# Half of a merge gate by seven block products, woven into the chunks of the next projection

## The chip, the cores and the metric

One core of a Trainium2 chip runs the whole kernel. The metric is the device time of one execution in microseconds, as a median of several. TensorE (PE in the profile, with PEld for its weight loads) multiplies; VectorE (DVE), ScalarE (ACT) and GpSimd (POOL) do the rest; SyncE (SP) issues most transfers, POOL those that add to what lies in SBUF.

## What is computed

One layer of an encoder block, 256 tokens, width 2048, float32:

```python
z = xn @ w_in[l]
u_lru, g_lru, q, k, v, g_attn, m_lru, m_attn = jnp.split(z, split_at, axis=-1)
...
y_a = h.astype(x.dtype) * jax.nn.silu(g_lru)
...
y_b = windowed_gqa(q, k, v, attn_sink[l]) * jax.nn.silu(g_attn)
merged = (jax.nn.sigmoid(m_lru) * (y_a @ w_proj_a[l])
          + jax.nn.sigmoid(m_attn) * (y_b @ w_proj_b[l]))
x = x + rms_norm(merged @ w_out[l], norm_post_w[l])
```

All matrices are 2048 high; w_in is 13312 wide, the others 2048. The change concerns m_attn, the attention's merge gate, which are the last 2048 columns of w_in.

## The kernel before, in words

Every float32 operand of a product is split into a high part rounded to fp32r (wh, written by ScalarE) and a low part, the rest (wl, by VectorE); a product is then three matmuls, high by high, high by low, low by high (`mm3`, L228 to L230). The weights come from DRAM in pieces of 128x2048 (1024 KB), one per step. `load_plan` lists the steps in order. A step has two half steps, each with one 128x1024 half of a piece.

Four kinds of steps there are. A "quad" is a quarter of the 2048 rows for a chunk of 512 output columns: 24 matmuls of 128x512 for the 256 tokens (`add_rows`). A "blk" makes columns on partitions (`add_pair`). A "part" is a step of the seven products: a 2x2 block of matrices is multiplied with seven products of sums of blocks instead of eight products of blocks (`Seven`, table `SEVEN`). Here the rows of the blocks are the two halves of the tokens (or of the 2048 inner rows, as pairs of 128), the columns two neighbouring chunks of 512. Each product has two steps of 12 matmuls. So 1024 output columns are 8 quads (192 matmuls) or 14 parts (168).

A product of seven needs sums on both sides. Sums of the left operand's blocks are made by VectorE (`sums_of`: four sums s1 to s4 of a pair unit, in fp32r parts of 128x4x2x128). Sums of the weights are made by transfers: a cell in SBUF is loaded with one block (`start`, by SP), and further blocks are added into it by POOL's accumulating transfers (`second`, and for m6, m7 and m4 in `fetch`, five steps ahead of use). Blocks are only added there; what has to be subtracted is in the left operand's sums and in the last additions (`after`). The products m1 and m2 use plain blocks, loaded like any other piece.

The order of the work is the order in which the code records it, half step by half step, in the loop at the end of `body`. At half step n the loop issues transfers (`fetch`, three steps ahead), runs what is due there (`at`, `soon`), splits the high part four half steps ahead and the low part three ahead (`split`), runs `behind` work, and records the half step's matmuls. Each engine then takes its own instructions in that order and waits by semaphores. Pieces have 3 buffers (raw), split halves 5, so ScalarE's cast for half step n+4 waits until TensorE has done half step n-1. Larger tiles share 34 slots of 4 KB per partition (`unit`).

The stages, in order: the inner branches' inputs (u, gl, ga) with the recurrence, k and v, then the heads stage: per group of four heads two q pairs and one chunk of MID (ml's second half and w_proj_a), while scores, softmax and values of the group before are woven in. After that comes the gate stage: four chunks of ma (m_attn, `gate_evac` applies the sigmoid) and four of pb (w_proj_b, `add_pb`). After a pb chunk VectorE multiplies by the gate and adds the other branch, two `turn`s transpose the result on TensorE, and its parts and their sums are made for w_out. w_out's stage takes its first two chunks by seven products, woven with the quads of chunks 2 and 3 in the order of `OUT`.

The lines that the prediction speaks of: L211 raw loads, L190 adding transfers and L192 plain cell loads, L223 high parts, L225 low parts, L313 to L315 sums, L156 low parts of activations, L785 to L806 softmax and transposes of p, L855 and L856 the evacuation of pb, L867 transposes of a turn.

Of the kernel before, what the change touches and what calls it, by code (L numbers as in the profile page):

```python
# [14 lines left out]
F32 = mybir.dt.float32  # L15
F32R = mybir.dt.float32r
AF = mybir.ActivationFunctionType
ALU = mybir.AluOpType
# [37 lines left out]
}  # L56


OUT = ("2.0 m1.0 2.1 m1.1 2.2 m5.0 m5.1 m3.0 2.3 m3.1 m6.0 m6.1 3.0 m2.0 m2.1 m7.0 3.1 m7.1 m4.0 m4.1 3.2 3.3").split()


PV_NORM = 0
# [9 lines left out]
def load_plan():  # L72

    plan = []

    def quad(m, c):
        plan.extend(("quad", m, c, i) for i in range(4))

    def pair(m, c, n):
        plan.extend(("blk", m, c + (n + i) * P, 0) for i in range(2))  # L80

    def mixed(m, c, order):
        for o in order:
            a, i = o.split(".")
            plan.append(("part", m, c, a, int(i)) if a in SEVEN else ("quad", m, c + int(a) * 512, int(i)))

    quad("w_in", U0)
    for i in range(8):
        if i in EARLY:
            quad("w_in", ML0 + EARLY.index(i) * 512)  # L90
        pair("w_in", GL0, 2 * i)
        pair("w_in", GA0, 2 * i)
        if i < 6:
            pair("w_in", U0, 2 * i + 4)
    pair("w_in", K0, 0)
    pair("w_in", K0, 2)
    quad("w_in", V0)
    for i in range(4):
        pair("w_in", Q0, 4 * i)
        pair("w_in", Q0, 4 * i + 2)  # L100
        quad(*MID[i])
    for m, c in MID[4:]:
        quad(m, c)
    for c in range(4):
        quad("w_in", MA0 + c * 512)
    for c in range(4):
        quad("w_proj_b", c * 512)
    mixed("w_out", 0, OUT)
    return plan

# [13 lines left out]
def body(ctx, tc, x, xT, wall, wlru, pvec, npost, ident_d, mask_d, rope_d, out):  # L124
# [3 lines left out]
    ring = ctx.enter_context(tc.tile_pool(name="ring", bufs=3))  # L128
    small = ctx.enter_context(tc.tile_pool(name="small", bufs=2))
    psum = ctx.enter_context(tc.tile_pool(name="psum", bufs=4, space=PSUM))  # L130
    ctx.enter_context(tc.manual_schedule())

    def unit(name, dt=F32, shape=(P, 4, S)):
# [5 lines left out]
    def banks(name, shape=(P, 2, 2, S)):  # L139
        return psum.tile(list(shape), F32, tag="mm", name=name, bufs=2)  # L140

    def half_unit(name, tag, dt=F32, bufs=2):
        return small.tile([P, 2, S], dt, tag=tag, name=name, bufs=bufs)
# [21 lines left out]
    def at(hs, fn):  # L165
        assert hs >= now[0], (hs, now[0])
        due.setdefault(hs, []).append(fn)
# [3 lines left out]
    def behind(hs, fn):  # L171
        last[hs] = fn
# [4 lines left out]
    def soon(fn, d=1):  # L177
        at(now[0] + d, fn)
# [125 lines left out]
    def sums_of(name, src, sums, psum):  # L304
        a = src.rearrange("p a b -> p (a b)")
        a11, a12, a21 = (a[:, i * P:(i + 1) * P] for i in (0, 2, 1))
        ends = src.rearrange("p a (b c) -> p (a b) c", b=2)[:, 0:4:3]
        f = half_unit(f"{name}f", "uu", F32).rearrange("p a (b c) -> p (a b) c", b=2)
        t = unit(name, F32R, (P, 4, 2, P))
        sums.append(t)  # L310

        def make(a21):
            nc.vector.tensor_tensor(f[:, 0:2], ends, a21.unsqueeze(1).to_broadcast([P, 2, P]), ALU.subtract)  # L313
            nc.vector.scalar_tensor_tensor(f[:, 2], f[:, 1], -1.0, a11, ALU.mult, ALU.subtract)
            nc.vector.scalar_tensor_tensor(f[:, 3], f[:, 2], -1.0, a12, ALU.mult, ALU.subtract)  # L315
            soon(lambda: parts_of(t[:, :, 0], t[:, :, 1], f))

        if psum:

            nc.scalar.copy(f[:, 3], a21)  # L320
            soon(lambda: make(f[:, 3]))
        else:
            make(a21)

    class Seven:

        def __init__(self, name, m, c, act, sums, done):
            self.name, self.act, self.sums, self.done = name, act, sums, done  # L330
            self.weights, self.cells, self.ps = ("part", m, c), {}, {}
            groups[m, c] = self

# [19 lines left out]

        def half(self, m, q, h, wh, wl):
            fresh, last = q == 0 and h == 0, q == 1 and h == 1
            if fresh and m in ("m5", "m3"):

                if m == "m5":
                    self.double = banks(f"{self.name}{m}", (P, 2, 512))
                self.ps[m] = self.double[:, int(m == "m3")]  # L360
            elif fresh:
                self.ps[m] = bank(f"{self.name}{m}", (P, 512))
            for j in range(2):
                ah, al = self.rows(SEVEN[m][0], 4 * q + 2 * h + j)
                sl = slice(j * 512, (j + 1) * 512)
                mm3(self.ps[m], ah, al, wh[:, sl], wl[:, sl], fresh and j == 0, last and j == 1)
            if last:
                soon(lambda: self.after(m))
# [4 lines left out]
        def after(self, m):  # L373
            ps, done = self.ps, self.done
            if m == "m1":
                self.m1 = small.tile([P, 512], F32, tag="upad", name=f"{self.name}c", bufs=2)
                nc.scalar.copy(self.m1, ps.pop("m1"))
            elif m == "m2":
                done(0, 0, ps.pop("m2"), self.m1, 1)
            elif m == "m6":  # L380

                self.u = self.temp("u")
                nc.vector.tensor_tensor(self.u, ps.pop("m6"), self.m1, ALU.add)
                v = self.temp("v")
                nc.vector.tensor_tensor(v, ps["m5"], self.u, ALU.add)
                done(0, 1, ps.pop("m3"), v, -1)
            elif m == "m7":

                nc.vector.tensor_tensor(self.u, ps.pop("m7"), self.u, ALU.add)
                done(1, 1, ps.pop("m5"), self.u, -1)  # L390
            elif m == "m4":
                done(1, 0, ps.pop("m4"), self.u, 1)
# [299 lines left out]
            scaled(dst, ps, lambda: soon(sigmoid))  # L692
        return done

    tm, sm, ms, msum = {}, {}, [], []


    def gate_evac(gates, c):
        def done(t, ps):
            if c not in gates:  # L700
                gates[c] = unit(f"mg{c}", F32, (P, 2, 512))
            nc.scalar.activation(gates[c][:, t], ps, AF.Sigmoid, scale=rtok[:, t:t + 1])
        return done
# [127 lines left out]
    def yb_parts(q):  # L831
        yb[q] = pair_unit(f"yb{q}")
        n = q % 2 * 2
        parts_of(yb[q][:, :, 0], yb[q][:, :, 1], sga[q // 2][:, n:n + 2])

    def heads(g):
        def then(h, l):
            b = now[0] + HEAD0
            for j in range(4):
                if j % 2 == 0:  # L840
                    both = {}
                head(4 * g + j, h, l, b + 4 * j, both)
        return then
# [8 lines left out]
    def add_pb(c):  # L852
        def done(t, ps):
            g = sm[c][:, t]
            nc.vector.tensor_tensor(g, ps, g, ALU.mult)  # L855
            nc.vector.tensor_tensor(g, tm[c][:, t], g, ALU.add)  # L856
            if t == 1:
                for i in range(2):
                    soon(lambda i=i: turn(i), i + 1)

        def turn(i):

            ps = bank(f"mt{c}{i}")
            for j in range(2):
                sl = slice((2 * i + j) * P, (2 * i + j + 1) * P)
                for t in range(2):
                    nc.tensor.transpose(ps[:, j, t * P:(t + 1) * P], sm[c][:, t, sl], ident)  # L867
            m = pair_unit(f"ms{2 * c + i}")
            ms.append(m)
            parts_of(m[:, :, 0], m[:, :, 1], ps)  # L870
            sums_of(f"mx{2 * c + i}", ps, msum, True)

        add_rows(f"pb{c}_", yb, done)

    def add_mixed(seven, order, classic):
        left = {}
        for o in order:
            a, i = o.split(".")
            if a in SEVEN:
                seven.add(a, int(i))  # L880
                continue
            if i == "0":
                n = len(steps)
                classic(int(a))
                left[a] = steps[n:]
                del steps[n:]
            steps.append(left[a].pop(0))
# [10 lines left out]
    for m, c in MID:  # L898
        mid.append((add_pa, c // 512) if m == "w_proj_a" else (add_ml, (c - ML0) // 512))
    for i in range(4):  # L900
        add_heads(f"q{i}", heads(i))
        f, n = mid[i]
        f(n)
    for f, n in mid[4:]:
        f(n)

    b = 2 * len(steps)
    for q in range(8):
        at(b + 12 + q, lambda q=q: yb_parts(q))
    for c in range(4):  # L910
        add_rows(f"ma{c}_", xs, gate_evac(sm, c))
    for c in range(4):
        add_pb(c)


    npt, xr, yw = [], [[], []], [[], []]
# [65 lines left out]
    for q in range(2):  # L982
        at(b - 16 + 4 * q, lambda q=q, s=seven: s.start("x", q))
        at(b - 12 + 4 * q, lambda q=q, s=seven: s.second(q))
        at(b - 4 + 4 * q, lambda q=q, s=seven: s.start("y", q))
    add_mixed(seven, OUT, lambda c: add_rows(f"o{c}_", ms, lambda t, ps: o_done(t, c, ps), c == 3, c == 3))


    assert [s[0] for s in steps] == [p[0] for p in plan]
# [91 lines left out]
```

## Time and profile before

| | |
|---|---|
| median of 3 runs | 904.9 us (904.82 to 905.37) |
| the profiled execution | 905.53 us, span 903.7 us, mean granted clock 0.997 |
| matmuls, busy share of TensorE | 4638, 99% |
| busy share of VectorE, ScalarE | 75%, 61% |
| transfers | 180.59 MB, mean 200 GB/s |
| ma's four chunks | from 633.7 to about 721 us |
| pb's four chunks | from about 723 to 815 us |

The page tells busy times per engine, slices of the span, transfer queues, the chain of waits and the costliest groups. A group's row reads: line, engine, operation, what is written and read, shape and count, then busy time and mean ns, then the idle time before it and who ended it. A windows row gives busy time and count per engine in a stretch, then the clock, the share of the 16 transfer engines and GB/s.

### The profile page before, as it was taken

The numbers are of one execution on the slowest core, as the hardware profiler recorded it, in microseconds if no ns is written. First come the engines' busy times: TensorE is split into PE (matmuls) and PEld (weight loads), VectorE is DVE, ScalarE is ACT, GpSimd is POOL, SyncE is SP. The second block draws the span as 40 slices with busy tenths as digits, with TensorE's granted clock in tenths as the row PEclk, the third lists the DMA queues.
The fourth block names the chain that finished last, engine by engine and source line by source line (L and its number), as shares of the span: only waits on it lengthen the run. The fifth ranks groups of instructions, "written<-read, shape, count | busy, mean of one in ns | idle before, by whom it ended". The sixth has DMA issues, their size and how long they took to land.

```text
span 903.7 us, 12068 instructions
## 1 busy us (share of the span) xinstructions
PE 893.5 (99%) x4638; PEld 765.8 (85%) x4638; DVE 678.0 (75%) x947; ACT 555.5 (61%) x777; POOL 16.8 (2%) x40
## 2 busy tenths in 40 slices
PE   8999999999999999999999999999999999999996
PEld 8888888888898888888888888888888888888885
DVE  6897978696979889896687868656555447778686
ACT  7688586958687977844555544654455444445764
POOL 0000000000000000000000000000000000101200
PEclk9999999999999999999999999999999999999998
DMA  9764555546455454555544444535555556988992
GB/s 339 251 241 170 191 206 198 197 145 212 176 215 196 159 205 150 199 210 187 187 170 157 163 164 141 185 140 186 187 187 186 186 186 227 289 303 274 223 314 93
DMA packets 30778, 180.59 MB, mean 200 GB/s; under 512 B 3424, under 2 KB 4192, under 8 KB 12160
## 3 DMA queue, kind: packets, MB, share of 16 engines
q1 hardware_dynamic: 27840, 170.67, 52.7%
q0 software_dynamic: 2304, 8.39, 4.9%
q10 hardware_dynamic: 576, 0.76, 0.3%
q8 instruction: 36, 0.59, 0.2%
q14 instruction: 22, 0.18, 0.1%
HBM read 177.71 MB, written 2.10 MB: 199 GB/s over the span
## 4 chain that ended last, share of the span: by engine, by line
PE 98%; DMA 0%; DVE 0%; ACT 0%; DVEq 0%; issue 0%; SPq 0%
PE q L255 6%; PE ga L255 6%; PE gl L255 6%; PE u L255 5%; PE gl L253 3%; PE ga L253 3%; PE q L253 3%; PE u_ps L509 3%; PE u L253 3%; PE k L255 2%; PE omm L229 1%; PE omm L230 1%; PE omm L228 1%; PE o L230 1%; PE o L228 1%; PE o L229 1%
## 5 line engine op out<-in xcount | busy, mean ns | idle before, releaser
L223 ACT CAST wh<-raw 128x1024 fp32r<-128x1024 f32 (+1 forms) x299 | 309.0, 1041 | 220.7 <-PE q L255 31.4
L225 DVE TENSOR_TENSOR wl<-raw,wh 128x1024 fp32r<-128x1024 f32 (+1 forms) x300 | 358.3, 1205 | 107.2 <-ACT wh L223 106.3
L255 PE MATMUL q<-xs,wh 128*128 128x512 f32 x256 | 62.8, 391 | 0.0
L255 PE MATMUL ga<-xs,wh 128*128 128x512 f32 x256 | 62.4, 391 | 0.0
L255 PE MATMUL gl<-xs,wh 128*128 128x512 f32 x256 | 62.4, 391 | 0.0
L255 PEld LDWEIGHTS gl<-xs,wh 128*128 128x128 f32 x256 | 46.9, 188 | 9.0
L255 PEld LDWEIGHTS ga<-xs,wh 128*128 128x128 f32 x256 | 46.9, 188 | 8.9
L255 PEld LDWEIGHTS q<-xs,wh 128*128 128x128 f32 x256 | 46.6, 188 | 8.8
L255 PE MATMUL u<-xs,wh 128*128 128x512 f32 x192 | 46.8, 391 | 0.0
L255 PEld LDWEIGHTS u<-xs,wh 128*128 128x128 f32 x192 | 35.2, 188 | 6.7
L253 PE MATMUL q<-xs,wl 128*128 128x256 f32 x256 | 34.4, 284 | 0.0
L253 PEld LDWEIGHTS q<-xs,wl 128*128 128x128 f32 x256 | 33.1, 191 | 1.2
L253 PEld LDWEIGHTS gl<-xs,wl 128*128 128x128 f32 x256 | 33.0, 191 | 1.2
L253 PEld LDWEIGHTS ga<-xs,wl 128*128 128x128 f32 x256 | 33.0, 191 | 1.3
L253 PE MATMUL gl<-xs,wl 128*128 128x256 f32 x256 | 33.7, 283 | 0.0
L253 PE MATMUL ga<-xs,wl 128*128 128x256 f32 x256 | 33.5, 283 | 0.0
L253 PEld LDWEIGHTS u<-xs,wl 128*128 128x128 f32 x192 | 24.8, 191 | 0.9
L253 PE MATMUL u<-xs,wl 128*128 128x256 f32 x192 | 25.2, 283 | 0.0
L608 DVE SCALAR_TENSOR_TENSOR uu<-upad,pv,uu 128x256 f32<-128x256 f32 x48 | 23.3, 485 | 2.3
L785 DVE CUSTOM_DVE_ANT_0 p<-sc,mask,pv 128x256 f32<-128x256 f32 x32 | 14.2, 478 | 9.9 <-PE sc L230 9.7
L631 ACT ACTIVATE gr<-gate,pv 128x256 f32<-128x256 f32 x32 | 15.3, 477 | 4.6 <-PE gate L230 4.6
L230 PE MATMUL gate<-ul,lwl 128*128 128x256 f32 x64 | 18.1, 283 | 0.0
(436 smaller groups left out, 2027.5 us busy)
## 6 DMA issues: line engine op xcount, KB each, us to landing
raw<-wall_dram SPq DMA_DIRECT2D x145, 1024.0 KB, 4.8
lraw<-wlru_dram SPq DMA_DIRECT2D x8, 512.0 KB, 5.7
raw<-wall_dram SPq DMA_DIRECT2D x8, 256.0 KB, 4.5
xr<-x_dram SPq DMA_DIRECT2D x4, 512.0 KB, 12.3
omx0a<-wall_dram POOLq DMA_DIRECT2D x3, 512.0 KB, 6.9
omx0b<-wall_dram POOLq DMA_DIRECT2D x3, 512.0 KB, 8.4
omx1a<-wall_dram POOLq DMA_DIRECT2D x3, 512.0 KB, 9.5
omx1b<-wall_dram POOLq DMA_DIRECT2D x3, 512.0 KB, 11.0
```

The lines of the kernel that those rows point to most:

```text
L223: cast(hs, raw)
L225: nc.vector.tensor_tensor(ls, raw, hs.bitcast(F32), ALU.subtract)
L228: nc.tensor.matmul(ps, wh, xh, start=start, stop=False)
L229: nc.tensor.matmul(ps, wh, xl, start=False, stop=False)
L230: nc.tensor.matmul(ps, wl, xh, start=False, stop=stop)
L253: nc.tensor.matmul(ps[:, 1], wl[:, sl], a[:, 0], start=False, stop=False)
L255: nc.tensor.matmul(ps, wh[:, sl], a, start=k == 0, stop=k == KT - 1)
L509: nc.tensor.matmul(ups[b // 2][:, b % 2, m], w[:, sl], a[:, n], start=k == 0 and w is wh and m == 0, stop=stop)
L608: nc.vector.scalar_tensor_tensor(u, up[:, j, tap:tap + S], cw[:, tap:tap + 1], u, ALU.mult, ALU.add)
L631: nc.scalar.activation(v["gr"][:, 2 * d + j], ps[:, 0], AF.Sigmoid, bias=pv[:, PV_BR + b:PV_BR + b + 1])
L785: nc.vector.tensor_tensor_reduce(p[:, t], sc[:, t], mask[:, t], P ** -0.5, sk, ALU.add, ALU.max, m[:, t:t + 1])
```

## The change

The upper half of m_attn (columns 1024 to 2047, ma's chunks 2 and 3) is now computed with seven products. Its 14 parts are woven with the quads of ma's chunks 0 and 1 and with those of all four pb chunks, in the order of the new list `GATE`. The left operand is x, whose eight pair units xs live through most of the kernel. The sums of their blocks are made in the heads stage (`x_sums`, two per group of heads), stored in DRAM and their slots given back; in the gate stage they are loaded again (`x_sums_back`), four and four. m5 and m3 of this group get a bank each instead of one double bank. The temporary u of `Seven` uses another buffer ring. The turns of pb's chunk 0 come ten half steps later.

```diff
+GATE = ("a0.0 a0.1 m1.0 a0.2 m1.1 a0.3 m2.0 a1.0 m2.1 a1.1 m5.0 m3.0 a1.2 a1.3 b0.0 m6.0 m7.0 b0.1 b0.2 m5.1 m3.1 "
+        "b0.3 b1.0 b1.1 m6.1 m7.1 b1.2 b1.3 b2.0 m4.0 m4.1 b2.1 b2.2 b2.3 b3.0 b3.1 b3.2 b3.3").split()
+CHUNKS = {"a": ("w_in", MA0), "b": ("w_proj_b", 0), "o": ("w_out", 0)}
...
-    for c in range(4):
-        quad("w_in", MA0 + c * 512)
-    for c in range(4):
-        quad("w_proj_b", c * 512)
+    mixed("w_in", MA0 + 1024, GATE)
     mixed("w_out", 0, OUT)
...
+    away = [dram.tile([P, 4 * 2 * P], F32, name=f"away{q}") for q in range(8)]
+    xsum = {}
+
+    def x_sums(q):
+        a = half_unit(f"xa{q}", "uu", F32)
+        nc.vector.tensor_tensor(a, xs[q][:, :, 0].bitcast(F32), xs[q][:, :, 1].bitcast(F32), ALU.add)
+        sums_of(f"xx{q}", a, xsum, False)
+        soon(lambda: nc.sync.dma_start(away[q], xsum.pop(q).rearrange("p a b c -> p (a b c)").bitcast(F32)), 3)
+
+    def x_sums_back(q):
+        xsum[q] = unit(f"xb{q}", F32R, (P, 4, 2, P))
+        nc.sync.dma_start(xsum[q].rearrange("p a b c -> p (a b c)").bitcast(F32), away[q])
...
-                self.u = self.temp("u")
+                self.u = small.tile([P, 512], F32, tag="upad", name=f"{self.name}u", bufs=2)
...
                 for i in range(2):
-                    soon(lambda i=i: turn(i), i + 1)
+                    soon(lambda i=i: turn(i), (10 if c == 0 else 1) + i)
...
     for i in range(4):
+        behind(2 * len(steps) + 14, lambda i=i: x_sums(2 * i))
+        behind(2 * len(steps) + 18, lambda i=i: x_sums(2 * i + 1))
         add_heads(f"q{i}", heads(i))
...
     b = 2 * len(steps)
+    seven = Seven("am", "w_in", MA0 + 1024, xs, xsum, lambda t, c, ps, *a: then(gate_evac(sm, 2 + c), t, combine(f"af{t}{c}", ps, *a)), False)
+    for q in range(2):
+        at(b + 18 * q, lambda q=q, s=seven: s.start("x", q))
+        at(b + 6 + 18 * q, lambda q=q, s=seven: s.second(q))
+        at(b + 10 + 22 * q, lambda q=q, s=seven: s.start("y", q))
     for q in range(8):
-        at(b + 12 + q, lambda q=q: yb_parts(q))
-    for c in range(4):
-        add_rows(f"ma{c}_", xs, gate_evac(sm, c))
-    for c in range(4):
-        add_pb(c)
+        at(b + 14 + q, lambda q=q: yb_parts(q))
+        at(b + 7 + q if q < 4 else b + 30 + q, lambda q=q: x_sums_back(q))
+    add_mixed(seven, GATE, lambda kind, c: add_rows(f"ma{c}_", xs, gate_evac(sm, c)) if kind == "a" else add_pb(c))
```

In the lists, a0.0 is the first quad of ma's chunk 0, b of pb, o of w_out; m5.1 is the second step of product m5.

SP's queue at the start of the gate stage, before: raw pieces, one behind the other.

```order
L211 DMA raw_5909<-wall_dram 128x2048
L211 DMA raw_5948<-wall_dram 128x2048
L211 DMA raw_5984<-wall_dram 128x2048
L211 DMA raw_6025<-wall_dram 128x2048
L211 DMA raw_6064<-wall_dram 128x2048
```

The same place now. amx and amy are the cells of the weights' sums, xb are the sums of x coming back.

```order
L198 DMA amx0a<-wall_dram 128x1024
L198 DMA amx0b<-wall_dram 128x1024
L217 DMA raw_6003<-wall_dram 128x2048
L217 DMA raw_6042<-wall_dram 128x2048
L217 DMA raw_6067<-wall_dram 128x2048
L343 DMA xb_6087<-away_74 128x1024
L217 DMA raw_6112<-wall_dram 128x2048
L343 DMA xb_6114<-away_75 128x1024
L343 DMA xb_6127<-away_76 128x1024
L217 DMA raw_6139<-wall_dram 128x2048
L198 DMA amy0a<-wall_dram 128x1024
L198 DMA amy0b<-wall_dram 128x1024
```

Cells and sums stand between the raw pieces, so a piece goes behind up to three of them.

VectorE behind pb's chunk 1, before: four evacuations (mg), then the two turns (ms, mx) with one split (wl) between them.

```order
L855 TENSOR_TENSOR mg_6182<-pb__6620,mg_6182 128x512
L856 TENSOR_TENSOR mg_6182<-mg_1446,mg_6182 128x512
L225 TENSOR_TENSOR wl_1_6768<-raw_6712,wh_1_6767 128x1024
L225 TENSOR_TENSOR wl_0_6794<-raw_6749,wh_0_6793 128x1024
L156 TENSOR_TENSOR ms_6815<-mt_6810,ms_6815 128x2x256
L313 TENSOR_TENSOR mx2f<-mt_6810,mx2f 128x256
L314 SCALAR_TENSOR_TENSOR mx2f<-mx2f,mt_6810 128x128
L315 SCALAR_TENSOR_TENSOR mx2f<-mx2f,mt_6810 128x128
L225 TENSOR_TENSOR wl_1_6821<-raw_6749,wh_1_6820 128x1024
```

And now:

```order
L162 TENSOR_TENSOR ms_6876<-mt_6871,ms_6876 128x2x256
L319 TENSOR_TENSOR mx1f<-mt_6871,mx1f 128x256
L320 SCALAR_TENSOR_TENSOR mx1f<-mx1f,mt_6871 128x128
L875 TENSOR_TENSOR mg_6444<-pb__6690,mg_6444 128x512
L876 TENSOR_TENSOR mg_6444<-mg_1456,mg_6444 128x512
L231 TENSOR_TENSOR wl_1_6886<-amx0b,wh_1_6885 128x1024
L162 TENSOR_TENSOR mx_6853<-mx0f,mx_6853 128x4x128
L231 TENSOR_TENSOR wl_0_6913<-amx1a,wh_0_6912 128x1024
L162 TENSOR_TENSOR mx_6879<-mx1f,mx_6879 128x4x128
L162 TENSOR_TENSOR ms_6936<-mt_6931,ms_6936 128x2x256
L319 TENSOR_TENSOR mx2f<-mt_6931,mx2f 128x256
L231 TENSOR_TENSOR wl_1_6942<-amx1b,wh_1_6941 128x1024
```

Chunk 0's turns (mx0f, mx1f) end just ahead of chunk 1's evacuation, their low parts stand behind it, and the splits there are m4's, whose half steps have half the matmuls.

VectorE in the heads stage, at the first `x_sums`, has five rows that were not there:

```order
L337 TENSOR_TENSOR xa_4030<-xs_132 128x512
L319 TENSOR_TENSOR xx0f<-xa_4030 128x256
L320 SCALAR_TENSOR_TENSOR xx0f<-xx0f,xa_4030 128x128
L321 SCALAR_TENSOR_TENSOR xx0f<-xx0f,xa_4030 128x128
L231 TENSOR_TENSOR wl_0_4027<-raw_3988,wh_0_4026 128x1024
L162 TENSOR_TENSOR xx_4033<-xx0f,xx_4033 128x4x128
```

They stand behind the splits of a half step; the low part xx follows one split later.

More of the change, by code (lines that the diff above doesn't have):

```diff
@@ L56 @@
 }
-OUT = ("2.0 m1.0 2.1 m1.1 2.2 m5.0 m5.1 m3.0 2.3 m3.1 m6.0 m6.1 3.0 m2.0 m2.1 m7.0 3.1 m7.1 m4.0 m4.1 3.2 3.3").split()
+GATE = ("a0.0 a0.1 m1.0 a0.2 m1.1 a0.3 m2.0 a1.0 m2.1 a1.1 m5.0 m3.0 a1.2 a1.3 b0.0 m6.0 m7.0 b0.1 b0.2 m5.1 m3.1 "
+        "b0.3 b1.0 b1.1 m6.1 m7.1 b1.2 b1.3 b2.0 m4.0 m4.1 b2.1 b2.2 b2.3 b3.0 b3.1 b3.2 b3.3").split()
+OUT = ("o2.0 m1.0 o2.1 m1.1 o2.2 m5.0 m5.1 m3.0 o2.3 m3.1 m6.0 m6.1 o3.0 m2.0 m2.1 m7.0 o3.1 m7.1 m4.0 m4.1 o3.2 o3.3").split()
+CHUNKS = {"a": ("w_in", MA0), "b": ("w_proj_b", 0), "o": ("w_out", 0)}
 PV_NORM = 0
@@ L84, in mixed @@
             a, i = o.split(".")
-            plan.append(("part", m, c, a, int(i)) if a in SEVEN else ("quad", m, c + int(a) * 512, int(i)))
+            if a in SEVEN:
+                plan.append(("part", m, c, a, int(i)))
+            else:
+                w, w0 = CHUNKS[a[0]]
+                plan.append(("quad", w, w0 + int(a[1]) * 512, int(i)))
     quad("w_in", U0)
@@ L130, in body @@
     psum = ctx.enter_context(tc.tile_pool(name="psum", bufs=4, space=PSUM))
+    dram = ctx.enter_context(tc.tile_pool(name="dram", bufs=1, space=bass.MemoryType.DRAM))
     ctx.enter_context(tc.manual_schedule())
@@ L309, in sums_of @@
         t = unit(name, F32R, (P, 4, 2, P))
-        sums.append(t)
+        sums[int(name[2:])] = t
         def make(a21):
@@ L323, in sums_of, with __init__ @@
             make(a21)
+    away = [dram.tile([P, 4 * 2 * P], F32, name=f"away{q}") for q in range(8)]
[8 more added lines that the diff above has]
+        nc.sync.dma_start(xsum[q].rearrange("p a b c -> p (a b c)").bitcast(F32), away[q])
     class Seven:
-        def __init__(self, name, m, c, act, sums, done):
-            self.name, self.act, self.sums, self.done = name, act, sums, done
+        def __init__(self, name, m, c, act, sums, done, double=True):
+            self.name, self.act, self.sums, self.done, self.double = name, act, sums, done, double
             self.weights, self.cells, self.ps = ("part", m, c), {}, {}
@@ L355, in half @@
             fresh, last = q == 0 and h == 0, q == 1 and h == 1
-            if fresh and m in ("m5", "m3"):
+            if fresh and self.double and m in ("m5", "m3"):
                 if m == "m5":
-                    self.double = banks(f"{self.name}{m}", (P, 2, 512))
-                self.ps[m] = self.double[:, int(m == "m3")]
+                    self.pair = banks(f"{self.name}{m}", (P, 2, 512))
+                self.ps[m] = self.pair[:, int(m == "m3")]
             elif fresh:
@@ L693, in silu_evac @@
         return done
-    tm, sm, ms, msum = {}, {}, [], []
+    tm, sm, ms, msum = {}, {}, [], {}
     def gate_evac(gates, c):
@@ L883, in add_mixed @@
                 n = len(steps)
-                classic(int(a))
+                classic(a[0], int(a[1]))
                 left[a] = steps[n:]
@@ L985, in body @@
         at(b - 4 + 4 * q, lambda q=q, s=seven: s.start("y", q))
-    add_mixed(seven, OUT, lambda c: add_rows(f"o{c}_", ms, lambda t, ps: o_done(t, c, ps), c == 3, c == 3))
+    add_mixed(seven, OUT, lambda _, c: add_rows(f"o{c}_", ms, lambda t, ps: o_done(t, c, ps), c == 3, c == 3))
     assert [s[0] for s in steps] == [p[0] for p in plan]
```

## The prediction, made before the result was known

> **What bounds the kernel now.** I read the page's busy times first, then the chain of waits, then the list of TensorE's own waits.
>
> ```profile
> PE 893.5 (99%) x4638; PEld 765.8 (85%) x4638; DVE 678.0 (75%) x947; ACT 555.5 (61%) x777; POOL 16.8 (2%) x40
> PEclk9999999999999999999999999999999999999998
> PE 98%; DMA 0%; DVE 0%; ACT 0%; DVEq 0%; issue 0%; SPq 0%
> PE u_ps L509 <- DVE wh L223: 1.1, 1, 1.1
> PE spin L406 <- POOL eps L402: 1.0, 1, 1.0
> PE u_ps L509 <- DVE xs L436: 0.5, 1, 0.5
> ```
>
> TensorE is busy for 99% of the span and is 98% of the chain. The three rows are all its waits, 2.6 us, and all lie at the start. The clock's digit is 9 in every slice but the last, the tail. So time is the number of products, and a product taken out counts in full as long as nothing else makes TensorE wait. Busy alone doesn't prove that products run at their best rate, so I take the rate from starts:
>
> ```profile
> L228 PE MATMUL ma__6035<-wh,xs x32: 389/389/389, 657.3 to 678.4; 128*128 128x512 f32 x32
> L228 PE MATMUL ma__6339<-wh,xs x32: 389/389/389, 700.8 to 721.9; 128*128 128x512 f32 x32
> 700.00:710.00 10.00, 10.00 (x46) 8.29 (x45) 4.27 (x4) 5.15 (x6) 0.00 (x0) 1.00 0.61 211
> 840.00:850.00 10.00, 10.00 (x46) 8.29 (x45) 6.13 (x5) 5.46 (x7) 3.12 (x4) 1.00 1.06 255
> ```
>
> Two chunks later the same product starts 700.8 - 657.3 = 43.5 us later. That is 192 products, so 226.6 ns each (the 389 ns are overlapped). The last two rows (PE, PEld, DVE, ACT, POOL, clock, DMA share, GB/s) are 10 us of ma's chunks and 10 us of w_out's stage, which already uses seven products: 46 products in both. A product in a part step costs no more than one in a quad.
>
> **The change, part by part.** I call a step's 24 products on a 512-column chunk a quad (24 x 0.2266 = 5.44 us), and a step of the seven products a part (12, 2.72 us).
>
> *Removed from TensorE.* ma's last two chunks were 8 quads, 192 products. They become 14 parts, 168. The order confirms 24 rows fewer. 24 x 0.2266 = **5.44 us**. Transposes and everything else on TensorE stay.
>
> *Sums of x, in the heads.* Eight times there are, on VectorE, a 128x512 add, a 128x256 subtraction, two 128x128 and a 128x512 low part; on ScalarE one cast; on SP a 512 KB store.
>
> ```profile
> L856 DVE TENSOR_TENSOR mg<-mg,mg 128x512 f32<-128x512 f32 x8 | 5.5, 692 | 0.3
> L313 DVE TENSOR_TENSOR mx5f<-mt,mx5f 128x256 f32<-128x256 f32 x1 | 0.4, 416 | 0.0
> L314 DVE SCALAR_TENSOR_TENSOR mx1f<-mx1f,mt 128x128 f32<-128x128 f32 x1 | 0.3, 289 | 0.0
> L156 DVE TENSOR_TENSOR yb<-sg,yb 128x512 fp32r<-128x512 f32 x8 | 5.5, 684 | 0.0
> L155 ACT CAST yb<-sg 128x512 fp32r<-128x512 f32 x8 | 5.0, 620 | 0.0
> 440.00:600.00 160.00, 160.00 (x838) 136.90 (x837) 122.66 (x232) 84.67 (x144) 0.00 (x0) 1.00 0.47 165
> ```
>
> A piece is 0.69 + 0.42 + 2 x 0.29 + 0.68 = 2.37 us of VectorE and 0.62 us of ScalarE, so 19.0 and 5.0 us in all. VectorE has 160 - 122.7 = 37 us free in this window alone. What counts is lateness. Closest to TensorE stands the normalising of p before its transposes:
>
> ```profile
> 636.60 0.62 DVE L800 TENSOR_SCALAR p<-p,rd 128x256 f32<-128x256 f32 x2
> 641.83 0.60 PE L806 MATMUL pt<-ident,p 128*128 128x128 f32 x4
> ```
>
> p is ready 641.83 - 637.22 = 4.6 us ahead. A piece comes apart in 1.7 and 0.7 us, so its 2.4 us fit. I take 0. Without that cover the price would be up to 19 us (every piece in full). The store on SP waits for a VectorE instruction that stands ahead of the low part for which the next load waits anyway, so it holds no load back. Its bytes go through an engine share of 0.47.
>
> *Transfers in the gate stage.*
>
> ```profile
> q1 hardware_dynamic: 27840, 170.67, 52.7%
> q0 software_dynamic: 2304, 8.39, 4.9%
> raw<-wall_dram SPq DMA_DIRECT2D x145, 1024.0 KB, 4.8
> 655.00:677.00 22.00, 22.00 (x98) 18.21 (x97) 12.57 (x13) 11.84 (x15) 0.00 (x0) 1.00 0.54 182
> 820.00:860.00 40.00, 40.00 (x178) 32.98 (x177) 30.45 (x31) 26.99 (x32) 9.55 (x11) 1.00 1.01 265
> ```
>
> A 1024 KB load takes 0.527 x 903.7 us x 1.049 / 170.67 = 2.93 us of the 16 engines. An accumulating 512 KB load (q0, 16 of them) takes 0.049 x 903.7 / 16 = 2.77 us. Before, the stage had 32 loads, 94 us in 174 (0.54, as the row at 655 shows). Now it has 28 raw loads, 4 MB into cells, 4 MB of sums back and 16 adds: 36 x 2.93 + 16 x 2.77 = 150 us in 168.6, a share of 0.89. The stage of w_out holds 1.01 over 40 us with TensorE never waiting (last row), so the mean is no obstacle. The tightest stretch is the first: up to the start of a1.1 TensorE has 5 quads and 4 parts, 38.1 us. By then SP has 7 raw loads, 2 MB of cells and 2 MB of sums ahead of it, and POOL two adds: 11 x 2.93 + 2 x 2.77 = 37.8 us. Loads start some 3 us before the stage (an estimate: one waits for the split of the third step back, which runs about three half steps ahead), and the last needs 1.9 us more to land (4.8 - 2.93) and 2.3 us to be split. That balances to about -1 to +3 us of waiting: below nothing is impossible, as TensorE has no wait there to lose. I take 0, since neither the adds nor the y cells are needed before m5.0 and m3.0, and keep 3.
>
> In the Trainium skill, "DMA: Bandwidth & Descriptors", section "Anatomy of one DMA — SWDGE (gpsimd) path", a transfer issued by GpSimd costs about 2.0 us fixed and the rest at 436 GB/s. By it an estimate for one add's movement is 1.2 us instead of 2.77, the stage's sum would be 125 us, and the first stretch would fit with 3 us to spare. The trace speaks against it: adds land later.
>
> *Waits that SP gets.* The second four sums go into slots that the first three free in m7.0, so SP stands there until TensorE has read them. Behind it are the raw loads of b0.3, b1.0 and b1.1. From the last such read to b1.0's cast, at m3.1, TensorE runs 0.7 + 2 x 5.44 + 2.72 = 14.3 us. The queue needs 3 x 2.93 + 1.9 = 10.7 us for two sums, b0.3's load and b1.0's. Hidden, by 3.6 us.
>
> *The four turns.* b0's two turns now come ten half steps late, next to b1's, and after them m4's two parts, whose halves are half as long.
>
> ```profile
> L225 DVE TENSOR_TENSOR wl<-raw,wh 128x1024 fp32r<-128x1024 f32 x165 | 199.5, 1219 | 78.9 <-ACT wh L223 78.5
> L855 DVE TENSOR_TENSOR mg<-pb__6620,mg 128x512 f32<-128x512 f32 x2 | 1.4, 688 | 3.1 <-PE pb__6620 L230 3.1
> L867 PE MATMUL mt<-ident,mg 128*128 128x128 f32 x32 | 5.7, 279 | 0.0
> ```
>
> From the end of b1 until the low part of b2.1's first half, VectorE does four evacuations (2.76), four splits (4.88), b1's two turns (2 x 1.68) and two low parts of b0's sums (1.37): 12.4 us. TensorE in that time runs 2 halves of b1.2's kind (5.44), 4 part halves (5.44) and eight transposes (5.7 us of busy for 32, so up to 1.4): 12.1 to 12.3 us, reading a low part one product late, 0.2. So it waits 0 to 0.3 us. If b0's turns aren't done by then, up to 1.7 more, one turn. I take 0.2. The evacuations of the gate's four pieces (2.1 and 1.4 us at most at a time) find halves enough; the rest is equal work elsewhere.
>
> The sum: profiled execution 905.53 us (span 903.7), minus 5.44, plus 0.2, gives 900.3. The median, 904.9, lies 0.6 below that execution, so it becomes **899.7 us**. The range of this case is 899.0 to 901.0.
>
> **Rivals.** *Transfers don't fit the first stretch.* For: 37.8 us of movement in 38.1, and adds that share engines with loads. Against: w_out's stage at 1.01. It gives back about 2.3 us (middle of 1 and 3.6): 902.0. In the Trainium skill the same page, "Issuing engines are not separate DMA queues", says that queues of all issuers run on the same 16 engines; by that rule POOL's adds come out of the loads' time, which is this rival. The trace agrees in the share of 1.01 with 265 GB/s.
>
> *VectorE falls behind* at the turns or in the heads. For: the 12.4 us above. Against: free time at both places. A turn late is 1.7 us: 901.4.
>
> *Slower: the chained adds land too late.* m6, m7 and m4 are each made by adding into a cell that the product before has just been read from.
>
> ```profile
> DMA to landing us min/median/max: 7.2/9.7/13.5
> ```
>
> These are omx1b's three adds. In the gate an add has, from m5's split to m6's cast, m3 and three quads, 2.72 + 16.3, less one half: 17.7 us (in w_out 12.2). Past that, every us late is a us of waiting, at m6 and m7 of each half, two rounds. It takes a landing of 18 us before anything is lost, and 21.3 to lose 2 x 3.6 us and be slower: about 907. The longest here is 13.5.
>
> *It doesn't do what it says:* parts that run like quads would add 14 x 2.72 = 38 us; the rows of 46 products exclude all but extra waiting per part. About 904 to 906, no change.
>
> **How the numbers follow.** Forecast 0.69; first rival 0.15; second 0.07; adds 0.05; the last 0.04. A measurement of this kernel tells 0.2% (1.8 us) from no change: faster is below 903.1, slower above 906.7. Of the first rival a part reaches no change. Faster 0.69 + 0.12 + 0.06 = 0.87, same 0.07, slower 0.06. The range goes from 898.9 (all 5.44 and 0.5 of spread) to 902.9 (3 us of waiting beside the forecast).
>
> **What would show it.** TensorE with 4614 products, and no row of its waits beyond the three and a few tenths at mt or omm. A share of DMA near 0.9 from 634 to 800, with raw loads there landing at 6 to 9 us. VectorE's window 440 to 600 near 0.85, ScalarE's casts there still released by TensorE. A wait of amm's or ma's products on a cast released by a DMA, in the first 40 us of the gate, makes the first rival; a wait at b2.1, the second; at m6 or m7, the third. Any of them over 3.6 us in sum makes the prediction wrong, as does a wait in the heads.

## The result, and the profile after

The changed kernel took 900.0 us, the median of four executions (899.5 to 901.1), where the kernel before took 905.1 beside it (four executions). The ratio is 0.9944, with a 95% interval from 0.9927 to 0.9961. The forecast was 899.7, so a gain of 5.1 us stands where 5.2 was predicted. The profiled execution took 899.96 us, with a span of 898.2.

The page of the changed kernel: busy times, granted clock by slices, share of the chain by engine.

```profile
PE 888.4 (99%) x4614; PEld 761.6 (85%) x4614; DVE 712.8 (79%) x1006; ACT 572.4 (64%) x798; POOL 30.7 (3%) x56
PEclk9999999999999999999999999999999999999999
PE 98%; DMA 1%; DVE 0%; ACT 0%; SPq 0%; DVEq 0%; issue 0%
```

All of TensorE's waits in it (total, times, longest):

```profile
PE spin L426 <- POOL eps L422: 1.0, 1, 1.0
PE u_ps L529 <- DVE wh L229: 0.9, 1, 0.9
```

There are 24 products less, 5.1 us less of TensorE's busy time (893.5 before), and still no wait behind the start. All the new work lies beside TensorE: VectorE has 35 us more, ScalarE 17, POOL 14.

The same kernel by stretches (PE, PEld, DVE, ACT, POOL, clock, DMA share, GB/s): the heads, two pieces of the gate's first stretch, and the gate stage.

```profile
440.00:600.00 160.00, 160.00 (x838) 136.95 (x837) 134.72 (x262) 88.01 (x150) 0.00 (x0) 1.00 0.53 187
...
633.00:655.00 22.00, 22.00 (x101) 18.19 (x100) 14.69 (x18) 9.30 (x10) 1.79 (x2) 1.00 0.92 295
655.00:677.00 22.00, 22.00 (x99) 18.22 (x98) 15.79 (x17) 17.93 (x23) 1.40 (x2) 1.00 0.96 371
640.00:800.00 160.00, 160.00 (x719) 131.94 (x718) 115.58 (x130) 91.84 (x109) 15.67 (x18) 1.00 0.94 297
```

The last stretch before the change, for its share of the transfer engines:

```profile
640.00:800.00 160.00, 159.99 (x718) 131.75 (x717) 93.23 (x108) 76.66 (x93) 3.67 (x4) 1.00 0.63 212
```

VectorE in the heads went from 122.7 to 134.7 us of 160, and the transfer engines in the gate stage from 0.63 to 0.94. TensorE is busy in all of it.

How near the new work came to TensorE is not in the waits, since there are none. It is read from the end of a low part on VectorE and the start of the first product that reads it. VectorE at m4's last half (from the cell amx1b) and at the first half of b2.1:

```profile
763.94 1.22 DVE L231 TENSOR_TENSOR wl<-amx1b,wh 128x1024 fp32r<-128x1024 f32 x1
...
766.66 1.22 DVE L231 TENSOR_TENSOR wl<-raw,wh 128x1024 fp32r<-128x1024 f32 x1
```

TensorE's products that read them:

```profile
766.95 0.39 PE L235 MATMUL amm<-wl,xs 128*128 128x512 f32 x1
...
768.31 0.39 PE L235 MATMUL pb__6916<-wl,yb 128*128 128x512 f32 x1
```

The leads are 766.95 - 765.16 = 1.8 us and 768.31 - 767.88 = 0.4 us. The second is the tightest place of the gate stage: read in the same way, b2.1's second half has 1.4 us, and every other half step that is not shown here 2.2 or more. It is also the place at which the prediction took 0.2 us of waiting.

### The profile page after: what moved, and what is told of

The parts are those of the page before. It is cut to its first block, busy times and chain, and to the rows that moved or that the text cites. A ratio compares the mean times of both kernels' runs of the same rounds, so it can differ in the third digit from the quotient of the medians.

```text
span 898.2 us, 12207 instructions
## 1 busy us (share of the span) xinstructions
PE 888.4 (99%) x4614; PEld 761.6 (85%) x4614; DVE 712.8 (79%) x1006; ACT 572.4 (64%) x798; POOL 30.7 (3%) x56
## 4 chain that ended last, share of the span: by engine, by line
PE 98%; DMA 1%; DVE 0%; ACT 0%; SPq 0%; DVEq 0%; issue 0%
PE q L261 7%; PE ga L261 7%; PE gl L261 7%; PE u L261 5%; PE gl L259 3%; PE ga L259 3%; PE q L259 3%; PE u L259 3%; PE u_ps L529 2%; PE k L261 2%; PE omm L235 1%; PE omm L236 1%; PE amm L235 1%; PE amm L236 1%; PE omm L234 1%; PE amm L234 1%
## 5 line engine op out<-in xcount | busy, mean ns | idle before, releaser
L229 ACT CAST wh<-raw 128x1024 fp32r<-128x1024 f32 (+1 forms) x291 | 300.0, 1041 | 178.9 <-PE q L261 25.6
L231 DVE TENSOR_TENSOR wl<-raw,wh 128x1024 fp32r<-128x1024 f32 (+1 forms) x292 | 348.1, 1204 | 67.8 <-ACT wh L229 65.3
L259 PE MATMUL q<-xs,wl 128*128 128x256 f32 x256 | 34.4, 284 | 0.0
L235 PE MATMUL gate<-ul,lwh 128*128 128x256 f32 x64 | 18.1, 283 | 0.0
```

The lines of the kernel that those rows point to most:

```text
L229: cast(hs, raw)
L231: nc.vector.tensor_tensor(ls, raw, hs.bitcast(F32), ALU.subtract)
L235: nc.tensor.matmul(ps, wh, xl, start=False, stop=False)
L259: nc.tensor.matmul(ps[:, 1], wl[:, sl], a[:, 0], start=False, stop=False)
```

## The experiments

**Where the gain comes from: sums alone, the count alone, and the sums' cost.** The first kernel makes, stores and loads back the sums of x and does nothing with them; the gate is made of quads as before.

```diff
-    mixed("w_in", MA0 + 1024, GATE)
+    for c in range(4):
+        quad("w_in", MA0 + c * 512)
+    for c in range(4):
+        quad("w_proj_b", c * 512)
...
-    add_mixed(seven, GATE, ...)
+    for c in range(4):
+        add_rows(f"ma{c}_", xs, gate_evac(sm, c))
+    for c in range(4):
+        add_pb(c)
```

> The kernel before with the sums of x alone: made in the heads, stored, loaded again in the gate stage, and read by nothing; the gate by plain quads, 4638 products. My theory (time is the number of products, the sums are hidden): the time of before, 905.1 us, ratio 0.999 to 1.001, no new wait of TensorE. Rival (the sums cost time in the heads, and the change's gain is net of it): up to 19 us of VectorE's work shows, 906 to 924.

It took 904.89 us (11 executions), and the kernel before, beside it, 904.89; the ratio is 0.9998 (0.9989 to 1.0007). The sums by themselves cost nothing that shows; the interval leaves room for 0.6 us. (The kernel before had medians of 904.9 to 905.3 on the occasions of these runs, so a few tenths of a microsecond between runs of different occasions tell nothing.)

The second kernel is the changed one without the work on VectorE and ScalarE for the sums: the same slots, store and loads, but what is stored is x's unit itself.

```diff
-        a = half_unit(f"xa{q}", "uu", F32)
-        nc.vector.tensor_tensor(a, xs[q][:, :, 0].bitcast(F32), xs[q][:, :, 1].bitcast(F32), ALU.add)
-        sums_of(f"xx{q}", a, xsum, False)
-        soon(lambda: nc.sync.dma_start(away[q], xsum.pop(q)...), 3)
+        soon(lambda: nc.sync.dma_start(away[q], xs[q]...), 3)
```

> The change without the sums' work on VectorE and ScalarE: xs itself is stored and loaded in place of its sums, so the transfers, the products and the order stay, and half of the gate is computed from wrong sums. My theory: the time of the change, 900.0 us (899.5 to 900.5), since the 19 us of VectorE were hidden. Rival (they were paid): below 899.4.

It took 899.85 us (5 executions; ratio 0.9942, 0.9930 to 0.9955), against 900.0 with the work. So the work in the heads is hidden from this side too.

The third gives the 24 products back: in pb's last chunk one product of three matmuls in each half step is done twice.

```diff
-                mm3(got[t], a[:, 0], a[:, 1], wh[:, sl], wl[:, sl], k == 0, k == KT - 1)
+                if name == "pb3_" and t == 0 and j == 0:
+                    mm3(got[t], a[:, 0], a[:, 1], wh[:, sl], wl[:, sl], k == 0, False)
+                    mm3(got[t], a[:, 0], a[:, 1], wh[:, sl], wl[:, sl], False, False)
+                else:
+                    mm3(got[t], a[:, 0], a[:, 1], wh[:, sl], wl[:, sl], k == 0, k == KT - 1)
```

> The change with 24 products put back: in pb's chunk 3 one set of three per half step is done twice, so that chunk's result is wrong. 4638 products as before. My theory: 24 x 0.2266 = 5.4 us more than the change, 905.4 us, the time of before. Rival (part of the 5.1 us comes from the new order or from the start): 901 to 904.

It took 904.58 us (11 executions; ratio 0.9996, 0.9987 to 1.0005). The busy times of this kernel:

```profile
PE 894.3 (99%) x4638; PEld 767.6 (85%) x4638; DVE 713.0 (79%) x1006; ACT 572.5 (63%) x798; POOL 30.7 (3%) x56
```

All of TensorE's waits in it:

```profile
PE spin L430 <- POOL eps L426: 1.0, 1, 1.0
```

TensorE's busy time is back where it was, and with it 4.6 of the 5.1 us. So some nine tenths of the gain are shown to be the count. The sum would have been 5.4, to 905.4. The 0.8 us that are missing stay open: the profiled executions differ by 0.9 us in their waits at the start (1.9 in the changed kernel, 1.0 here), but one execution of each doesn't prove that this is the gap.

**How much more the heads would carry.** The first add of each sum of x is done four times, or nine times, instead of once: 2.1 or 5.5 us more of VectorE per piece by the rows' 0.69 us, 1.9 or 5.2 by its busy time (727.8 and 754.4 us against 712.8, over eight pieces), since neighbours overlap a little.

```diff
+        for _ in range(4):    # the other kernel: 9
             nc.vector.tensor_tensor(a, xs[q][:, :, 0].bitcast(F32), xs[q][:, :, 1].bitcast(F32), ALU.add)
```

> The change with the first add of each of the eight sums done four times instead of once: 2.1 us more per piece, 16.6 us of VectorE more in the heads. My theory: in 440 to 600 us VectorE has 25 us free and low parts are 6 us or more ahead, so nothing: 900.0 us. Rival (the heads are close to waiting on VectorE): 902 to 917.

> The same with nine times instead of once: 5.5 us more per piece, 44 us in all, two pieces (11 us) per group of 51.6 us in which VectorE has 8.2 us free. My theory: this is past the cover, VectorE falls behind by some 3 us per group and TensorE waits for it: 903 to 910 us. Rival (bursts don't matter, or free time elsewhere takes them up): 900.0.

With four it took 899.67 us (4 executions; ratio 0.9941, 0.9926 to 0.9956), with nine 916.58 (4; ratio 1.0126, 1.0111 to 1.0141). The window of the heads with four adds:

```profile
440.00:600.00 160.00, 160.00 (x838) 136.93 (x837) 148.75 (x285) 89.27 (x152) 0.00 (x0) 1.00 0.52 188
```

The same with nine, and the stretch behind it:

```profile
440.00:600.00 160.00, 152.26 (x787) 128.92 (x786) 155.67 (x293) 74.61 (x136) 0.00 (x0) 0.99 0.47 167
600.00:634.00 34.00, 30.26 (x137) 24.74 (x136) 30.52 (x58) 19.27 (x29) 0.00 (x0) 0.95 0.58 207
```

TensorE's waits with nine, but for the one at the start:

```profile
PE pa__5591 L235 <- DVE wl L231: 3.7, 1, 3.7
PE o L235 <- DVE pl L162: 3.6, 2, 1.8
PE pt L827 <- DVE p L821: 2.4, 2, 1.5
PE q L259 <- DVE wl L231: 1.7, 2, 1.1
```

VectorE can be filled to 149 of 160 us and TensorE doesn't notice. The traces show why: from 440 to 620 us the shortest leads in the changed kernel are 6.8 us for a low part of weights and 5.4 for p, and with four adds these are the same, though longer ones have shrunk: VectorE has caught up where the leads are short.

At 156 TensorE does notice, in four kinds of place. p's transposes, which the prediction watched as the closest, are only one of them and wait 2.4 us of 11.4; the low parts of weights (pa and q) wait 5.4. My expectation for nine adds, 903 to 910, was too small. The direction was right, but I had counted on the leads to take more, and the waits are not the whole price: 914.5 - 898.2 = 16.3 us of span stand against 11.4 us of waits, and the clock in the last row is 0.95. Two stretches of 3.4 us in this trace have a clock of 0.50 (506.7 to 510.1 and 615.9 to 619.3), which is up to 3.4 us more; the last 1.5 us stay open. The next three runs ask what one late low part costs. The first of them was made before these two, the others after.

**What lateness costs at the tightest place.** Extra 128x512 adds on VectorE go in at m4's first half: eight, and later three and five.

```diff
+    def more():
+        t = half_unit("more", "p")
+        for _ in range(8):    # the others: 3, 5
+            nc.vector.tensor_tensor(t, xs[0][:, :, 0].bitcast(F32), xs[0][:, :, 1].bitcast(F32), ALU.add)
+
+    at(b + 58, more)
```

> The change with eight 128x512 adds more on VectorE at m4's first half step, 4.9 to 5.5 us, read by nothing. My theory: this is the tightest place, the low part of b2.1's first half is there 0.4 us ahead of TensorE, so all but that turns into waiting: 904.4 to 905.1 us, with a wait of omm-like products of amm or pb on wl. Rival (there is cover, as everywhere else, where 5 to 10 us lie ahead): 900.0.

With eight it took 905.73 us (10 executions; ratio 1.0012, 1.0003 to 1.0021). VectorE at that place, with the eight adds and the low part behind them:

```profile
761.72 5.77 DVE L939 TENSOR_TENSOR more<-xs 128x512 f32<-128x512 f32 x8
...
769.58 1.22 DVE L231 TENSOR_TENSOR wl<-amx1b,wh 128x1024 fp32r<-128x1024 f32 x1
```

TensorE there, start and duration; in brackets the wait:

```profile
770.85 0.80 PE L235 MATMUL amm<-wl,xs 128*128 128x512 f32 x1 [3.79 <-DVE wl L231]
771.44 0.63 PE L236 MATMUL amm<-wh,xs 128*128 128x512 f32 x1
771.87 0.63 PE L234 MATMUL amm<-wh,xs 128*128 128x512 f32 x1
...
775.86 0.48 PE L234 MATMUL pb__6916<-wh,yb 128*128 128x512 f32 x1
```

The window of these 10 us (the last three numbers are clock, DMA share and GB/s):

```profile
770.00:780.00 10.00, 9.15 (x29) 7.11 (x30) 9.93 (x14) 6.39 (x8) 0.00 (x0) 0.70 0.39 116
```

The time is above the 904.4 to 905.1 that I expected. The wait of 3.8 us is what the lead predicts: 8 x 0.69 - 1.8 = 3.7. But after it products start every 427 ns, not every 227. From 770.85 to 775.86 there are eleven intervals (two of them, with some 0.6 us, are longer still), 5.01 us where 2.49 are normal, so 2.5 us more. Wait and slow products make 6.3 of the 6.5 us by which the span is longer than the changed kernel's (904.7 against 898.2).

This is the profiled execution, 906.43 us, and not a typical one: it and two others of the ten had a mean clock of 0.993 or 0.994 and took 906.4 to 907.8, the other seven had 0.996 and took 905.1 to 905.9. So the price of the slow products differs from one execution to the next: against the changed kernel's 900.0, and beyond the wait of 3.8 us, seven lose 1.3 to 2.1 us and three 2.6 to 4.0.

In the Trainium skill, "TensorE: Matmul & The Clock Gate", section "What's actually happening", the array falls to half its clock after an idle window of about 3.4 us; section "HAM oscillation — how this bites in real kernels" tells the same of kernels that wait longer than that. The trace agrees, in the 427 ns and in the 0.70 granted over 10 us. With the nine adds in the heads it does not agree throughout: there the slow products came once behind a wait of 1.8 us, as the rows below show.

If it takes so long a wait, a shorter one must cost its own length and no more. Two more runs ask for it, with three adds and with five.

> As the eight extra adds, with three: 2.1 us more VectorE work at m4's first half. Theory (the leads of the low parts, read from the changed kernel's trace, are 1.8 us at m4's second half and 0.4 at b2.1's first; a wait costs its own length): waits of 0.3 us at amm and 1.3 at b2.1's pb, 1.6 in sum, so 901.6 us. Rival (whatever VectorE is late counts in full): 902.1. Rival (the leads are not the bound, the eight adds cost through the clock alone): no wait, 900.0.

> Five extra adds, 3.5 us more VectorE work at m4's first half. With eight adds TensorE waited 3.8 us once, and then eleven products came at intervals of 427 instead of 227 ns, under a lower granted clock: some 2.5 us more. Theory (a wait counts its own length, and the slow products come only behind a wait of over 2 us or so): waits of 1.7 us at amm and 1.3 at b2.1, 3.0 in sum, no slow products, so 903.0 us. Rival (any wait of over a microsecond is followed by slow products): 2.5 us more behind the first, in which the second wait vanishes: 1.7 + 2.5, so 904.2. Rival (slow products go with the sum late): 905 or more.

Three adds took 901.30 us (5 executions; ratio 0.9961, 0.9948 to 0.9973), five 903.13 (11; ratio 0.9978, 0.9969 to 0.9987). The waits at this place with three adds:

```profile
PE pb__6916 L235 <- DVE wl L231: 1.1, 1, 1.1
...
PE amm L235 <- DVE wl L231: 0.2, 1, 0.2
```

With five adds:

```profile
PE amm L235 <- DVE wl L231: 1.6, 1, 1.6
PE pb__6916 L235 <- DVE wl L231: 1.1, 1, 1.1
```

The window of the same 10 us with five:

```profile
770.00:780.00 10.00, 9.10 (x40) 7.55 (x41) 9.55 (x10) 6.70 (x8) 0.00 (x0) 1.00 0.58 206
```

Two waits at the two named places, near the lengths that the leads give (0.3 and 1.3; 1.7 and 1.3), and the clock stays at 1.00. The times are 1.3 and 3.1 us above the changed kernel's, where the theory had 1.6 and 3.0. So the leads of the changed kernel's trace are a price list: up to 0.4 us of lateness there is free, then each us costs a us, and with a wait of 3.8 us another 1.3 to 4.0 are lost at once. Where exactly that begins is open. With the nine adds in the heads, products also slowed behind a shorter wait, which came 3 us after one of 1.1. The last row is an equal wait in the same trace, 3 us after one of 0.7, and there they didn't:

```profile
506.79 0.79 PE L235 MATMUL o<-pl,vh 128*128 128x512 f32 x1 [1.81 <-DVE pl L162]
507.38 0.63 PE L236 MATMUL o<-ph,vl 128*128 128x512 f32 x1
...
562.88 0.50 PE L235 MATMUL o<-pl,vh 128*128 128x512 f32 x1 [1.81 <-DVE pl L162]
563.22 0.39 PE L236 MATMUL o<-ph,vl 128*128 128x512 f32 x1
```

The five adds' 1.6 and 1.1 us, about as close together in the other order, were not followed by it either. So the length of one wait doesn't decide alone.

**How much more the transfers of the first stretch would carry.** One or three copies of 1 MB from DRAM to DRAM are put into SP's queue at half step 6 of the gate stage (counted from 0).

```diff
+    spare = [dram.tile([P, 2048], F32, name=f"spare{q}") for q in range(3)]
...
+    for q in range(3):    # the other kernel: range(1)
+        at(b + 6, lambda q=q: nc.sync.dma_start(spare[q], wall[q]))
```

> The change with one DRAM-to-DRAM copy of 1024 KB more on SP's queue, seven half steps into the gate stage's tightest stretch for transfers, just ahead of the first sums. My theory: 2.9 us or somewhat more of the 16 engines; the low parts of a1.1 and a1.2 are there 3.4 and 3.1 us ahead, so nothing or a few tenths: 900.0 to 900.5 us. Rival (transfers were far from limiting): 900.0 here and in the next run.

> The same with three such copies, 8.8 us or more of the engines. My theory: loads behind them come that much later, 3.1 to 5 us of it is covered, the rest is waiting of TensorE on casts released by raw loads, once: 903.5 to 906 us. Rival (transfers were far from limiting): 900.0.

One copy: 900.35 us (4 executions; ratio 0.9948, 0.9933 to 0.9962). Three: 904.01 (10; 901.8 to 905.7; ratio 0.9985, 0.9975 to 0.9995). With one copy the second piece of the stretch was full, and TensorE still didn't wait:

```profile
655.00:677.00 22.00, 22.00 (x98) 18.21 (x97) 14.91 (x16) 17.54 (x23) 0.86 (x1) 1.00 1.01 403
```

With three, ScalarE's cast for a1.1 (profiled execution: 901.77 us, the shortest of the ten):

```profile
673.03 1.04 ACT L229 CAST wh<-raw 128x1024 fp32r<-128x1024 f32 x1 [3.81 <-DMA raw<-wall_dram]
```

The products behind it:

```profile
674.12 0.50 PE L234 MATMUL ma__6219<-wh,xs 128*128 128x512 f32 x1 [1.25 <-ACT wh L229]
675.38 0.50 PE L235 MATMUL ma__6219<-wl,xs 128*128 128x512 f32 x1 [0.76 <-DVE wl L231]
```

This is the first rival, made to happen: the load of a1.1 lands late, ScalarE waits for it, TensorE for ScalarE. It comes at the place that the prediction named, a1.1, but only with more bytes. a1.1's load landed 13.8 us after its issue, where the changed kernel has 9.6. By their packets the three copies took 8.2 us of the 16 engines in this execution (2.5 for the single one). It lost some 2 us, the median 4.0, the longest 5.7. So the changed kernel has some 4 to 6 us of engine time to spare here, and 2.5 at the least. That takes the loss as lateness alone; the slower executions also have a lower clock (0.995 or 0.996 against 0.997 or 0.998), so a part of theirs can be slow products.

## Why the prediction was right, point by point

**The count** (5.44 us): right as the cause, and within some tenths as a size. TensorE's busy time fell by 5.1 us, the median by 5.1, and giving the products back returned 4.6.

**Sums in the heads, taken at 0**: right, by three runs (sums alone, no work for the sums, and 1.9 us more per piece without a loss). VectorE's window came to 134.7 of 160, 0.84, where near 0.85 was said. The work itself was smaller than said: 16.4 to 16.7 us of VectorE's busy time (712.8 - 696.4 without it in the changed kernel, 694.7 - 678.0 with it in the kernel before) instead of 19.0. The argument was weaker than its outcome. The lead of 4.6 us at p's transposes was read at 641.8 us, and the changed kernel makes its last sum at 587.6, so the sums don't touch that place: it has 4.6 us still. In the heads p's leads are 5.4 us or more. And with 5.2 us more per piece the low parts of weights, which the argument left out, lost more than p.

**Transfers, taken at 0**: the outcome was right, its reason mis-sized in two terms. The share over the stage was 0.94 instead of 0.89. The gate's own counts in the sum were right, as the queues' and the loads' rows show:

```profile
q1 hardware_dynamic: 30720, 179.06, 54.9%
q0 software_dynamic: 4608, 16.78, 9.9%
raw<-wall_dram SPq DMA_DIRECT2D x141, 1024.0 KB, 4.8
```

An adding transfer took 0.099 x 898.2 / 32 = 2.78 us of the 16 engines, as before. What the sum left out is the next stage: w_out's first cells are loaded and added to before the gate stage ends. Two of the rows of the issues from 640 to 800 us:

```profile
omx0a<-wall_dram SPq DMA_DIRECT2D x1, 512.0 KB, 4.1
omx0a<-wall_dram POOLq DMA_DIRECT2D x1, 512.0 KB, 6.7
```

There are six such plain loads, 3 MB, and four adds, by the sum's prices 3 x 2.93 + 4 x 2.77 = 19.9 us. The gate's own issues in the window (26 raw loads, 7 MB of cells and sums, 14 adds) are 135.5 us by the same prices, so 0.85 of 160 without w_out's and 0.97 with them; 0.94 lies near the second. The kernel before has them too: its row from 640 to 800 shows 0.63, where the prediction's 0.54 for the stage was compared with 22 us early in it. Raw loads issued there landed after 4.7 to 15.7 us, 7.8 in the median, where 6 to 9 was said.

The second term is the margin of the first stretch, -1 to +3 us of waiting by my ledger, +1 in the middle. The trace shows a1.1's low part 3.4 us early, so it was some 4 us better. SP's queue in the changed kernel at the first two cells' loads and at a1.1's load (the first of the two in the last row), then the split and the first product of a1.1 that reads it:

```profile
625.74 0.43 SPq L198 DMA_DIRECT2D amx0a<-wall_dram  x1
626.26 0.38 SPq L198 DMA_DIRECT2D amx0b<-wall_dram  x1
...
658.32 4.41 SPq L217 DMA_DIRECT2D raw<-wall_dram  x2
...
669.07 1.23 DVE L231 TENSOR_TENSOR wl<-raw,wh 128x1024 fp32r<-128x1024 f32 x1 [1.10 <-ACT wh L229]
...
673.68 0.39 PE L235 MATMUL ma__6213<-wl,xs 128*128 128x512 f32 x1
```

The stage's first product starts at 633.5. The load landed 9.6 us after its issue, at 667.9, which is 34.4 us into the stage; the ledger has it at -3 + 37.8 + 1.9 = 36.7. It was 2.3 us too late there: 2 MB that it counted inside the stretch (the two cells and one raw load), 5.9 us by its price, were issued 7 to 8 us ahead of the stage, and it allowed 3 us for what went ahead. The rest is on TensorE's side: it came to a1.1 after 39.9 us instead of 38.1, because six products o and four transposes of p, left over from the heads, lie in the stretch too. By this the first rival's 0.15 was too much: it takes some 4 to 6 us more of transfers to make it happen.

**SP's wait for the slots of the second four sums**, hidden by 3.6 us: no wait of pb's second chunk stands in the list. No run tried it alone.

**The turns** (0.2 us): the place was right, the size not. The tightest low part comes 0.4 us ahead of its product instead of 0.2 us behind. The second rival was put at one turn, 1.7 us late; three adds, 2.1 us late, cost 1.3. A price of one us per us late holds for small sizes only. For anything that makes TensorE wait some 4 us the prediction lacked the slow products behind the wait.

**Chained adds too late**: not so. The gate's adds landed after 14.6 us at most (into amx0b; into amx1b 14.1), against the 17.7 that they have, and no wait stands at m6, m7 or m4.

**The median against the profiled execution**, 0.6 us below it: it was 0.0 here (900.0 and 899.96). The forecast for the profiled execution, 900.3, was 0.3 us too high and the one for the median, 899.7, as much too low. The four executions lie 1.6 us apart, so that the number came out within 0.3 us is in part luck; that it was some 5 us, and why, is not.

**The range** was given twice, 899.0 to 901.0 and 898.9 to 902.9. The working is that of the second, and its upper end adds up to 902.7 (899.7 and 3 us of waiting). The measured 900.0 lies in both.

No run points to a faster kernel of this shape: without any of the sums' work the time is the same, and TensorE has no wait left to take away.

## What to carry to other kernels

Where TensorE is busy for 99%, as here, a product taken out counts nearly in full (5.1 us of the 5.4 of 24 products), and the question is only whether the work that replaces it stays within the leads; these can be read as the time between the end of a split and the product that reads it, place by place, and they then say to a few tenths what a delay costs, as long as TensorE waits 1 or 2 us and not 4. A window's busy share doesn't tell that: VectorE at 93% cost nothing, at 97% 16 us. When loads are put into an already scheduled queue, look in the trace before you draw up a ledger of the stretch: which loads are issued ahead of it, what the next stage has put into it, and what else TensorE does in it.

## What the runs showed of the hardware

Waits of TensorE of 3.7 and 3.8 us were followed by products at about half their rate, 427 instead of 227 ns, at a granted clock of 0.50 for 3.4 us in the one trace and of 0.51 for 6.9 us in the other. Waits of 1.6 and 1.1 us, 2.7 us apart, were not. A wait of 1.8 us was, 3 us behind one of 1.1, and an equal one 3 us behind one of 0.7 was not. So a stall's price jumps, and two stalls of half the length can be cheaper than one, but no run here shows a length that is safe.

An adding transfer of 512 KB took 2.78 us of the 16 engines' time, a plain load of 1024 KB 2.93 in the kernel before, so an add costs about twice as much per byte.
